# A written order for VectorE and ScalarE in the feed-forward of a two-layer encoder, and out weights split one channel tile ahead

## The chip, the cores and the metric

The kernel runs on one core of one Trainium2 chip. The metric is device time in microseconds (us) of one execution. Engines in the profile: PE is TensorE's matmul, PEld its weight load, DVE is VectorE, ACT is ScalarE, POOL is GpSimd, and SP is SyncE, which sends the DMAs. Each engine has a queue of its own, and other engines release it by semaphores.

## The reference

Two layers work on 512 frames of 1024 channels in float32. Layer 0 mixes frames with causal pooling, layer 1 with chunked attention. Each is followed by the gated feed-forward that this document is about (d_ff = 2816):

```python
def conv_ffn(h, w_gate, w_val, conv_w, conv_b, w_out):
    S = h.shape[1]
    a = h @ w_gate
    ap = jnp.pad(a, ((0, 0), (CONV_W - 1, 0), (0, 0)))
    a = ap[:, 0:S] * conv_w[0] + ap[:, 1:S + 1] * conv_w[1] + ap[:, 2:S + 2] * conv_w[2] + conv_b
    return (jax.nn.silu(a) * (h @ w_val)) @ w_out
```

## The kernel before

**Tiles.** The hidden width is cut into 22 tiles of 128 rows (`NF`). Every operand of a matmul is split into a high part (ScalarE's copy, L98) and a low part (VectorE's subtraction, L99; both are the helper `split`), and a product adds high by high, high by low and low by high. `KIND` says how a tile is made: 0 and 1 early, 2 to 4 plainly, 5 to 21 with seven half-size products of a Strassen-Winograd form in place of eight. Tile 5 (`apart`) has a form of its own, tiles 6 and 7 are narrow, and tiles 8 to 21 are "wide": a high weight part multiplies both parts of the input in one matmul of 512 columns (L603), a low part the high part in one of 256 (L605).

**A seven-product tile** (`strassen`, L579) loads its gate and value weights g and v, and VectorE makes four sums s1 to s4 of their quarters (L583 to L586). Four weight tiles are split: g1 (g itself), g2 (s2 and s3), g3 (s1 and s4) and g4 (a quarter of v). The products go in the order b11, b21, t2, t3, t1, b22, t4 and accumulate in PSUM. Between them ScalarE copies PSUM out and VectorE adds: a for the gate (L618, L624, L657, L659), val for the value (L633, L648, L649, L663), with folds (L611) of the two halves that a wide matmul leaves. At the end `hidden` runs the convolution (L417 on ScalarE, two steps L419 on VectorE), the Silu (L420), the product with val (L664) and the split of the hidden rows into one of twelve slots.

**Out-projection.** The tiles are in four groups (`OUT`: 0 to 4, 5 to 10, 11 to 16, 17 to 21). When a group's tiles are done, `output(g)` multiplies its hidden rows by the out weights for eight channel tiles d (L119 to L121) and adds to X (L678). Its matmuls are spread in threes and fours behind the products of the next group's tiles. In it, the weights of d are loaded and split just ahead of the first matmul of d; two buffers hold the parts, one the raw load of the first three groups.

**What sets the order.** PE's order is written out (`manual_schedule` with PE): the list `order` puts b22 and t4 of a tile behind b11 and b21 of the next. VectorE, ScalarE and SyncE are placed in the feed-forward by a scheduler at build time, from a model of durations and from priorities that follow the text; `high_priority` raises the copies and sums behind t1. A few other places fix VectorE and ScalarE too, and there they run in the order of the text: the stretch from `frame_rstd` to the end of `blocks` in layer 0 is one.

**Buffers that matter.** Three raw weight loads (wr), two tiles for the sums (as), three pairs of weight parts in turn (`ring`), six scratch tiles (g), four PSUM banks for the products m and t, two for b and two for the out-projection.

Of the kernel before, what the change touches and what calls it, by code (L numbers as in the profile page):

```python
# [23 lines left out]
P = 128  # L24
# [27 lines left out]

KIND = "uuppp" + "s" * 17
WIDE = range(8, NF)
OUT = ((0, 5), (5, 6), (11, 6), (17, 5))
GM = 6
WAIT, HOLD = 2, 3
# [11 lines left out]
def trunk(ctx: ExitStack, tc: tile.TileContext, xt, xT, cols, band, edge, poolw, gv, wout, wqk, wv, wo, rel, out):  # L69
# [307 lines left out]
    def ffn(l, first, pool, acc, summed=None):  # L377
# [35 lines left out]
        def hidden(f, a, finish):  # L413

            cw = [col[:, C_CW[l] + 4 * f + j:C_CW[l] + 4 * f + j + 1] for j in range(4)]
            c = g_tile(f"c{f}")
            nc.scalar.activation(c, a, AF.Identity, scale=cw[2], bias=cw[3])  # L417
            for j in range(1, 3):
                nc.vector.scalar_tensor_tensor(c[:, j:], a[:, :S - j], cw[2 - j], c[:, j:], op0=OP.mult, op1=OP.add)  # L419
            silu = nc.scalar.activation(c, c, AF.Silu)  # L420
            if l == 0 and f == NF - 1:
                with tc.issue_after(silu.ins):
                    nc.scalar.preload_act_table_set("natural_log_exp_and_others")
            finish(c)
            split(c, *slot[f])

        def early():
# [39 lines left out]
            for f in range(n):  # L467
                a = pool.tile([P, S], F32, name=f"a{f}", tag="a", bufs=2)
                with tc.issue_after(made.ins):
                    nc.vector.tensor_mul(a, o[f, 0], R)  # L470

                def finish(c):
                    nc.vector.tensor_mul(c, c, R)
                    nc.vector.tensor_mul(c, o[f, 1], c)
                hidden(f, a, finish)
            return h, seed, known, made

        B, ready = {}, {}
# [33 lines left out]
        def plain(f):  # L512

            o = []
            for i in range(2):
# [10 lines left out]
                        yield mm  # L526
                if i == 0:
                    yield mm
            hidden(f, o[0], lambda c: nc.vector.tensor_mul(c, o[1], c))
            yield mm  # L530

        def apart(f):
# [42 lines left out]
            hidden(f, a, lambda c: nc.vector.tensor_mul(c, val, c))  # L575
            yield

        def strassen(f):

            g, v = (raw_tile(f"gv{l}_{f}_{i}", gv[l, f, i]) for i in range(2))  # L580
            sa, sb = (sum_tile(f"s{x}{f}") for x in "ab")
            a11, a12, a21, a22, s2, s3, s1, s4 = (x[:, z * S:(z + 1) * S] for x in (g, v, sa, sb) for z in range(2))
            nc.vector.tensor_add(s1, a21, a22)  # L583
            nc.vector.tensor_sub(s2, s1, a11)
            nc.vector.tensor_sub(s3, a11, a21)
            nc.vector.tensor_sub(s4, a12, s2)  # L586
            wide = f in WIDE
# [4 lines left out]
            def product(o, hl, z, name, first):  # L592
# [11 lines left out]
                for i, c in enumerate(cs):  # L604
                    nc.tensor.matmul(o[:, 0], lo[:, c], B[i, name][:, 0], start=False, stop=i == 3, **how)  # L605

            def flat(o):
                return o.rearrange("p c n -> p (c n)")

            def fold(out, x):  # L610
                nc.vector.tensor_add(out, x[:, :HALF], x[:, HALF:])  # L611

            a = pool.tile([P, S], F32, name=f"a{f}", tag="a", bufs=2)
            main, side = bank("S", "m"), bank("P", "b")
            w = parts(g, 1024, f"g1_{f}")
            product(main, w, 0, "b11", True)
            if wide:
                nc.scalar.activation(a, flat(main), AF.Copy)  # L618
            else:
                nc.scalar.activation(a[:, :HALF], main[:, 0], AF.Copy)  # L620
            yield
            product(side, w, 1, "b21", True)
            if wide:
                nc.vector.tensor_add(a, a, flat(side))  # L624
                fold(a[:, :HALF], a)
            else:
                nc.vector.tensor_add(a[:, :HALF], a[:, :HALF], side[:, 0])
            yield
            val = g_tile(f"v{f}")
            w = parts(sa, 1024, f"g2_{f}")  # L630
            product(main, w, 0, "t2", False)
            if wide:
                nc.scalar.activation(val, flat(main), AF.Copy)  # L633
                fold(val[:, :HALF], val)
            else:
                nc.scalar.activation(val[:, :HALF], main[:, 0], AF.Copy)
            yield
            side = bank("S", "t")
            product(side, w, 1, "t3", True)
            yield  # L640
            w = parts(sb, 1024, f"g3_{f}")
            last = [tmp.tile([P, S], F32R, name=f"g4_{f}_{c}", tag="g", bufs=6) for c in "hl"]
            split(a22, *last)
            product(main, w, 0, "t1", False)
            with tc.high_priority():
                if wide:
                    both_ = g_tile(f"w{f}")
                    nc.scalar.activation(both_, flat(main), AF.Copy)  # L648
                    nc.vector.tensor_add(both_, both_, flat(side))  # L649
                else:  # L650
                    nc.scalar.activation(val[:, HALF:], main[:, 0], AF.Copy)
                    nc.vector.tensor_add(val[:, HALF:], val[:, HALF:], side[:, 0])
            if wide:
                fold(val[:, HALF:], both_)
            yield
            product(main, w, 1, "b22", False)
            nc.scalar.activation(a[:, HALF:], main[:, 0], AF.Copy)  # L657
# [3 lines left out]
            product(side, last, 0, "t4", False)  # L661
            for c in range(2 if wide else 1):
                nc.vector.tensor_add(val[:, :HALF], val[:, :HALF], side[:, c])  # L663
            hidden(f, a, lambda c: nc.vector.tensor_mul(c, val, c))  # L664
            yield

        def output(g):

            b, m = OUT[g]
            n = m * P  # L670
            for d in range(KD):
                w = parts(raw_tile(f"wo{l}_{g}_{d}", wout[l, d, :, b * P:(b + m) * P], n, g + 1 < len(OUT)), n, f"ow{l}_{g}_{d}", True)
                o = psum("Q", f"out{l}_{g}_{d}")
                for i in range(m):
                    s = slice(i * P, (i + 1) * P)
                    yield from mm3(o, w[0][:, s], w[1][:, s], *slot[b + i], i == 0, i == m - 1)
                for fs in (slice(0, S),) if l == 0 or g < len(OUT) - 1 or d < KD - 1 else (slice(0, HALF), slice(HALF, S)):
                    nc.vector.tensor_add(X[d][:, fs], o[:, fs], X[d][:, fs])  # L678
                    if l == 1 and g == len(OUT) - 1:
                        nc.sync.dma_start(out[d * P:(d + 1) * P, fs], X[d][:, fs])  # L680

        with tc.manual_schedule(engines={mybir.EngineType.PE}):
            h, seed, known, made = early()
            queue, left, n = [], 0, 0
            order, prev = [], None
            for f in range(NF):
                if KIND[f] == "p":
                    order += [(f, j) for j in range(8)]
                if KIND[f] == "s" and KIND[f - 1] == "p":
                    order += [(f, j) for j in range(7)]  # L690
                elif KIND[f] == "s":
                    mine = [(f, j) for j in range(5)]
                    order += [x for j in range(2) for x in (mine[j], (prev, 5 + j))] + mine[2:] if prev else mine
                    prev = f
            order += [(prev, 5), (prev, 6)]
            steps = {f: (plain if KIND[f] == "p" else strassen if KIND[f - 1] == "s" else apart)(f) for f, _ in order}
            ends = [max(x for x, (f, _) in enumerate(order) if f == b + m - 1) + 1 for b, m in OUT]
            for g, (b, m) in enumerate(OUT):
                begin = ends[g - 1] if g else 0
                points = ends[g] - begin  # L700
                hold = HOLD * 3 * OUT[g - 1][1] if g == len(OUT) - 1 else 0
                todo = left
                for at, (f, _) in enumerate(order[begin:ends[g]], 1):
                    next(steps[f])
# [4 lines left out]
                    if at > WAIT:  # L709
                        due = (todo - hold) * (at - WAIT) // (points - WAIT)  # L710
                        while todo - left < due:
                            next(queue[0])
                            left -= 1
                if g:
# [336 lines left out]
```

## Time and profile before

| | us |
|---|---|
| time, median of 3 runs | 977.11 (977.01 to 979.12) |
| the profiled execution | 977.4 |
| its span, first to last instruction | 975.6 |
| granted TensorE clock | 0.999 |

A row of the timeline gives start, duration, engine, line, operation, out<-in and, in brackets, how long the engine had been idle and what released it. A row of a group gives the count, then the union of its busy time in us and the mean duration of one in ns, then idle time before its instructions with the releasers. A row of the waits gives total us, times, and the longest. A row of a stage gives, behind the stretch, its length, then busy us and the count of each engine. Two instructions of one engine can overlap in part, so that a start-to-start distance can be below a duration.

### The profile page before, as it was taken

What the parts mean: (1) busy time and instruction counts of PE and PEld (TensorE: products, weight loads), DVE (VectorE), ACT (ScalarE), POOL (GpSimd) and SP (SyncE); (2) the same over time, 40 slices, a digit from 0 to 9 for tenths busy, and PEclk for the clock granted to TensorE, in tenths of its full rate; (3) what the DMA queues carried; (4) which work ended last, traced back from release to release, by engine and by line L of the source; (5) the groups of instructions that cost most, each with busy time, mean ns of one, the idle gap of its engine ahead of it and who ended that gap; (6) DMA issues with size and microseconds to landing.
All of it is one profiled execution on the core that took longest, in us unless ns stands there. A gap on an engine that the chain in (4) does not pass through costs nothing.

```text
span 975.6 us, 13968 instructions
## 1 busy us (share of the span) xinstructions
PE 962.5 (99%) x5038; PEld 817.7 (84%) x5038; DVE 806.1 (83%) x1452; ACT 575.5 (59%) x990; POOL 103.2 (11%) x90
## 2 busy tenths in 40 slices
PE   8999999999999999999999999999999999999998
PEld 7788988788888888888888787888998878888886
DVE  8999989999989854442777887999999999989953
ACT  7665555555555444344898988646555555565521
POOL 2300000000000013203534532000000000000000
PEclk9999999999999999999999999999999999999999
DMA  9222233232322234233343341332324323333223
GB/s 340 71 98 92 92 114 114 79 123 95 113 83 96 73 84 150 87 120 96 108 117 107 96 118 54 100 108 79 114 92 130 118 78 119 91 105 104 80 68 112
DMA packets 37429, 102.84 MB, mean 105 GB/s; under 512 B 4432, under 2 KB 7904, under 8 KB 37360
## 3 DMA queue, kind: packets, MB, share of 16 engines
q1 hardware_dynamic: 37296, 101.90, 33.0%
q8 instruction: 40, 0.66, 0.3%
q14 instruction: 29, 0.24, 0.1%
q0 software_dynamic: 32, 0.04, 0.0%
q10 hardware_dynamic: 32, 0.00, 0.0%
HBM read 95.60 MB, written 2.14 MB: 100 GB/s over the span
## 4 chain that ended last, share of the span: by engine, by line
PE 90%; DVE 7%; ACT 2%; issue 1%; DMA 1%; SPq 0%; DVEq 0%; ACTq 0%
PE st_m L603 11%; PE out L120 8%; PE out L121 8%; PE out L119 8%; PE st_m L605 5%; PE st_t L603 5%; PE gv L120 3%; PE qk L120 3%; PE qk L119 3%; PE qk L121 3%; PE gv L121 3%; PE gv L119 3%; PE st_t L605 3%; PE st_b L603 2%; PE tp L882 2%; PE oo L894 2%
## 5 line engine op out<-in xcount | busy, mean ns | idle before, releaser
L120 PE MATMUL out<-one,ow_h 128*128 128x512 f32 x224 | 88.1, 393 | 3.7 <-DVE one L99 3.7
L121 PE MATMUL out<-one,ow_l 128*128 128x512 f32 x224 | 87.8, 392 | 0.0
L119 PE MATMUL out<-one,ow_h 128*128 128x512 f32 x224 | 87.8, 392 | 0.0
L98 ACT ACTIVATE ow_h<-wo_r 128x640 fp32r<-128x640 f32 (+1 forms) x64 | 50.5, 789 | 58.6 <-PE out L120 49.3
L678 DVE TENSOR_TENSOR X<-out,X 128x512 f32<-128x512 f32 (+1 forms) x65 | 44.1, 680 | 35.7 <-PE out L121 35.7
L603 PE MATMUL st_m<-two,g_h 128*128 128x512 f32 x224 | 70.0, 394 | 0.0
L603 PE MATMUL st_m<-h,g_h 128*128 128x512 f32 x224 | 69.0, 389 | 0.0
L98 ACT ACTIVATE g_h<-gv_r 128x512 fp32r<-128x512 f32 (+1 forms) x68 | 57.3, 842 | 16.3 <-PE st_b L603 10.6
L99 DVE TENSOR_TENSOR g_l<-gv_r,g_h 128x512 fp32r<-128x512 f32 (+1 forms) x68 | 64.9, 954 | 0.0
L99 DVE TENSOR_TENSOR ow_l<-wo_r,ow_h 128x640 fp32r<-128x640 f32 (+1 forms) x64 | 56.7, 886 | 2.6 <-ACT ow_h L98 2.6
L419 DVE SCALAR_TENSOR_TENSOR c<-a,col,c 128x511 f32<-128x511 f32 (+1 forms) x76 | 56.6, 747 | 1.8 <-ACT c L417 1.8
L98 ACT ACTIVATE g_h<-sb 128x1024 fp32r<-128x1024 f32 x34 | 36.0, 1060 | 28.4 <-PE st_m L603 25.7
L121 PE MATMUL qk<-wqk_h,two 128*128 128x512 f32 x128 | 51.4, 401 | 0.0
L119 PE MATMUL qk<-wqk_h,two 128*128 128x512 f32 x128 | 50.8, 409 | 0.0
L120 PE MATMUL qk<-wqk_l,two 128*128 128x512 f32 x128 | 50.8, 397 | 0.0
L120 PEld LDWEIGHTS out<-one,ow_h 128*128 128x128 f32 x224 | 42.4, 189 | 9.8 <-DVE one L99 4.6
L99 DVE TENSOR_TENSOR g_l<-sb,g_h 128x1024 fp32r<-128x1024 f32 x34 | 41.6, 1223 | 10.4 <-ACT g_h L98 10.4
L603 PEld LDWEIGHTS st_m<-h,g_h 128*128 128x128 f32 x224 | 42.1, 188 | 9.6
L603 PEld LDWEIGHTS st_m<-two,g_h 128*128 128x128 f32 x224 | 41.6, 188 | 10.0 <-ACT w L648 0.8
L605 PEld LDWEIGHTS st_m<-two,g_l 128*128 128x128 f32 x224 | 42.0, 188 | 8.8
L121 PEld LDWEIGHTS out<-one,ow_l 128*128 128x128 f32 x224 | 42.3, 189 | 6.3
L119 PEld LDWEIGHTS out<-one,ow_h 128*128 128x128 f32 x224 | 42.3, 189 | 6.1
(370 smaller groups left out, 2921.0 us busy)
## 6 DMA issues: line engine op xcount, KB each, us to landing
gv_r<-gv SPq DMA_DIRECT2D x86, 512.0 KB, 3.5
wo_r<-wout SPq DMA_DIRECT2D x32, 384.0 KB, 3.1
wo_r<-wout SPq DMA_DIRECT2D x32, 320.0 KB, 2.9
wqk_r<-wqk SPq DMA_DIRECT2D x16, 512.0 KB, 3.4
wv_r<-wv SPq DMA_DIRECT2D x8, 512.0 KB, 3.4
wo_r<-wo SPq DMA_DIRECT2D x8, 512.0 KB, 3.4
xt<-xt SPq DMA_DIRECT2D x4, 512.0 KB, 5.8
X<-xT SPq DMA_DIRECT2D x8, 256.0 KB, 7.4
```

Source lines behind the costliest of these rows:

```text
L98: nc.scalar.activation(hi, raw, AF.Copy)
L99: return (eng or nc.vector).tensor_sub(lo, raw, hi.bitcast(F32))
L119: yield nc.tensor.matmul(o, sh, mh, start=first, stop=False, **how)
L120: yield nc.tensor.matmul(o, sh, ml, start=False, stop=False, **how)
L121: yield nc.tensor.matmul(o, sl, mh, start=False, stop=last, **how)
L419: nc.vector.scalar_tensor_tensor(c[:, j:], a[:, :S - j], cw[2 - j], c[:, j:], op0=OP.mult, op1=OP.add)
L603: nc.tensor.matmul(o, hi[:, c], B[i, name], start=first and i == 0, stop=False, **how)
L605: nc.tensor.matmul(o[:, 0], lo[:, c], B[i, name][:, 0], start=False, stop=i == 3, **how)
L678: nc.vector.tensor_add(X[d][:, fs], o[:, fs], X[d][:, fs])
L882: nc.tensor.transpose(tp[:, j * P:(j + 1) * P], s_[:, j * P:(j + 1) * P], ident)
L894: nc.tensor.matmul(oo[:, j * P:], V[j, h // 4][:, h % 4].rearrange("p a d -> p (a d)"), PT[e][c][:, 4 * j:3 * j + TT].rearrange("p t q -> ...
```

## The change

**Order.** `strassen` is cut into sixteen steps. A new generator `tour` takes steps of three tiles in turn: o is the tile before, f the tile at hand, n the next. From the first place of tile 8 to the end of tile 21 VectorE and ScalarE are under `manual_schedule` too, so that they run in the order of the text. The out-projection's instructions that are traced in this stretch fall into that order behind one of the seven places. For a wide tile it comes to this:

| place | TensorE | VectorE, in order | ScalarE, in order |
|---|---|---|---|
| 0 | b11 of f | o: w add, w fold; f: s1, s2 | o: copy w |
| 1 | b22 of o | f: s3, s4 | f: copy a, g2 high |
| 2 | b21 of f | o: add second half of a; f: g2 low | o: copy second half of a, convolution start |
| 3 | t4 of o | f: a add, a fold; o: two convolution steps | f: g3 high; o: Silu |
| 4 | t2 of f | o: two val adds; f: g3 low | |
| 5 | t3 of f | f: val fold; o: product with val, hidden low | f: copy val; o: hidden high; n: g1 high |
| 6 | t1 of f | n: g1 low; f: g4 low | f: g4 high |

The loads of g and v of the next tile are traced at place 3. Tiles 6 and 7 take their steps in the same order, but the scheduler places them. `high_priority` is gone.

**Out weights.** `output` loads and splits the weights of channel tile d + 1 ahead of the matmuls of d, and those of its first channel tile as soon as its group is at hand.

```diff
+ORDERED = 8
...
             nc.scalar.activation(c, a, AF.Identity, scale=cw[2], bias=cw[3])
+            yield
             for j in range(1, 3):
                 nc.vector.scalar_tensor_tensor(c[:, j:], a[:, :S - j], cw[2 - j], c[:, j:], op0=OP.mult, op1=OP.add)
             silu = nc.scalar.activation(c, c, AF.Silu)
...
+            yield
             finish(c)
             split(c, *slot[f])
...
+            *w1, lo = parts(g, 1024, f"g1_{f}", later=True)
+            yield
+            lo()
+            yield
+            sa, sb = (sum_tile(f"s{x}{f}") for x in "ab")
+            a11, a12, a21, a22, s2, s3, s1, s4 = (x[:, z * S:(z + 1) * S] for x in (g, v, sa, sb) for z in range(2))
+            nc.vector.tensor_add(s1, a21, a22)
+            nc.vector.tensor_sub(s2, s1, a11)
+            main, side = bank("S", "m"), bank("P", "b")
+            product(main, w1, 0, "b11", True)
+            yield
             a = pool.tile([P, S], F32, name=f"a{f}", tag="a", bufs=2)
+            copy(a, main)
+            nc.vector.tensor_sub(s3, a11, a21)
+            nc.vector.tensor_sub(s4, a12, s2)
+            *w2, lo = parts(sa, 1024, f"g2_{f}", later=True)
+            yield
+            lo()
+            product(side, w1, 1, "b21", True)
+            yield
+            add(a, side)
+            fold(a[:, :HALF], a)
+            *w3, lo = parts(sb, 1024, f"g3_{f}", later=True)
+            yield
+            lo()
+            product(main, w2, 0, "t2", False)
             yield
             val = g_tile(f"v{f}")
+            copy(val, main)
+            fold(val[:, :HALF], val)
             side = bank("S", "t")
+            product(side, w2, 1, "t3", True)
+            yield
+            w4 = [tmp.tile([P, S], F32R, name=f"g4_{f}_{c}", tag="g", bufs=6) for c in "hl"]
+            split(a22, *w4)
+            product(main, w3, 0, "t1", False)
+            yield
+            x = g_tile(f"w{f}") if wide else val[:, HALF:]
+            copy(x, main)
+            add(x, side)
+            fold(val[:, HALF:], x)
+            yield
+            product(main, w3, 1, "b22", False)
+            yield
             nc.scalar.activation(a[:, HALF:], main[:, 0], AF.Copy)
             if wide:
                 nc.vector.tensor_add(a[:, HALF:], a[:, HALF:], main[:, 1])
+            gate = hidden(f, a, lambda c: nc.vector.tensor_mul(c, val, c))
+            next(gate)
+            yield
+            next(gate)
+            product(side, w4, 0, "t4", False)
+            yield
             for c in range(2 if wide else 1):
                 nc.vector.tensor_add(val[:, :HALF], val[:, :HALF], side[:, c])
+            yield
+            run(gate)
             yield
...
+            load(0)
+            yield
             for d in range(KD):
+                if d + 1 < KD:
+                    load(d + 1)
...
+                    now, new = new, strassen(f + 1) if f + 1 < NF else None
+                    for k, who in enumerate(("of", "fo", "of", "fon", "of", "fon", "nf")):
+                        if f == ORDERED and k == 0:
+                            order.enter_context(tc.manual_schedule(engines={ET.DVE, ET.Activation}))
+                        for x in who:
+                            if step := {"o": old, "f": now, "n": new}[x]:
+                                next(step)
+                        if old or k not in (1, 3):
+                            yield
+                    old = now
+            for k in range(6):
+                next(old)
+                if k in (1, 3):
+                    yield
+            order.close()
...
                 queue.append(output(g))
+                next(queue[0])
```

`parts(..., later=True)` gives the high part's copy at once and the low part's subtraction as a function to call later.

More of the change, by code (lines that the diff above doesn't have):

```diff
@@ L474, in finish @@
                     nc.vector.tensor_mul(c, o[f, 1], c)
-                hidden(f, a, finish)
+                run(hidden(f, a, finish))
             return h, seed, known, made
@@ L528, in plain @@
                     yield mm
-            hidden(f, o[0], lambda c: nc.vector.tensor_mul(c, o[1], c))
+            run(hidden(f, o[0], lambda c: nc.vector.tensor_mul(c, o[1], c)))
             yield mm
@@ L574, in apart @@
             nc.vector.tensor_add(val[:, :HALF], val[:, :HALF], product(w, 0, "t4"))
-            hidden(f, a, lambda c: nc.vector.tensor_mul(c, val, c))
+            run(hidden(f, a, lambda c: nc.vector.tensor_mul(c, val, c)))
             yield
         def strassen(f):
+            wide = f in WIDE
             g, v = (raw_tile(f"gv{l}_{f}_{i}", gv[l, f, i]) for i in range(2))
[L581 to L587, printed above, removed]
+            yield
             def bank(tag, name):
@@ L607, in flat, with fold @@
+            def fold(out, x):
+                if wide:
+                    nc.vector.tensor_add(out, x[:, :HALF], x[:, HALF:])
             def flat(o):
                 return o.rearrange("p c n -> p (c n)")
-            def fold(out, x):
-                nc.vector.tensor_add(out, x[:, :HALF], x[:, HALF:])
-            a = pool.tile([P, S], F32, name=f"a{f}", tag="a", bufs=2)
-            main, side = bank("S", "m"), bank("P", "b")
-            w = parts(g, 1024, f"g1_{f}")
-            product(main, w, 0, "b11", True)
@@ L629, in strassen @@
             val = g_tile(f"v{f}")
[L630 to L636, printed above, removed]
+            copy(val, main)
+            fold(val[:, :HALF], val)
+            side = bank("S", "t")
+            product(side, w2, 1, "t3", True)
             yield
-            side = bank("S", "t")
@@ L680, in output, with tour @@
                         nc.sync.dma_start(out[d * P:(d + 1) * P, fs], X[d][:, fs])
+        def tour():
+            for f in range(NF):
+                if KIND[f] == "p":
+                    yield from plain(f)
+                elif KIND[f] == "s" and KIND[f - 1] == "p":
+                    old, new = None, strassen(f + 1)
+                    for j, _ in enumerate(apart(f)):
+                        if j in (3, 5, 6):
+                            next(new)
+                        yield
+                elif KIND[f] == "s":
+                    now, new = new, strassen(f + 1) if f + 1 < NF else None
[13 more added lines that the diff above has]
+            order.close()
         with tc.manual_schedule(engines={mybir.EngineType.PE}):
@@ L684, in ffn @@
             queue, left, n = [], 0, 0
-            order, prev = [], None
+            order = ExitStack()
+            seq = []
             for f in range(NF):
[L687 to L697, printed above, removed]
+                if KIND[f] == "s" and KIND[f - 1] == "s":
+                    old = [[(f - 1, z)] if KIND[f - 2] == "s" else [] for z in (False, True)]
+                    seq += [(f, False), *old[0], (f, False), *old[1], *[(f, False)] * 3]
+                elif KIND[f] != "u":
+                    seq += [(f, z == 1) for z in range({"p": 8, "s": 7}[KIND[f]], 0, -1)]
+            seq += [(NF - 1, False), (NF - 1, True)]
+            ends = [seq.index((b + m - 1, True)) + 1 for b, m in OUT]
+            steps = tour()
             for g, (b, m) in enumerate(OUT):
-                begin = ends[g - 1] if g else 0
-                points = ends[g] - begin
+                points = ends[g] - (ends[g - 1] if g else 0)
                 hold = HOLD * 3 * OUT[g - 1][1] if g == len(OUT) - 1 else 0
                 todo = left
-                for at, (f, _) in enumerate(order[begin:ends[g]], 1):
-                    next(steps[f])
+                for at in range(1, points + 1):
+                    next(steps)
                     if n in range(3, 20, 5):
@@ L713, in ffn @@
                             left -= 1
+                if g == len(OUT) - 1:
+                    run(steps)
                 if g:
```

44 lines of the change are left out of this document (14 added, 30 removed).

## The prediction

> **What bounds the kernel now.** I began with the busy times and slices of the page.
>
> ```profile
> span 975.6 us, 13968 instructions
> ...
> PE 962.5 (99%) x5038; PEld 817.7 (84%) x5038; DVE 806.1 (83%) x1452; ACT 575.5 (59%) x990; POOL 103.2 (11%) x90
> ...
> PE   8999999999999999999999999999999999999998
> ...
> DVE  8999989999989854442777887999999999989953
> ```
>
> TensorE (PE) is busy 962.5 of 975.6 us and sets the time. VectorE (DVE) averages 83%, but the slices show that this mixes two things: 9 in both feed-forwards, 4 to 8 in the attention between them. So I asked for the stage that the change orders. In layer 0 it runs from the first matmul of tile 8 to the last of t1 of tile 21:
>
> ```profile
> 125.56 0.63 PE L603 MATMUL st_m<-two,g_h 128*128 128x512 f32 x2
> ...
> 332.72 0.40 PE L605 MATMUL st_m<-h,g_l 128*128 128x256 f32 x2
> ```
>
> Layer 1 has the same stretch 594 us later. Both as stages; columns: length, then busy time of PE, its weight load, DVE, ACT and POOL.
>
> ```profile
> 125.50:333.00 207.50, 205.65 (x1091) 176.36 (x1091) 191.89 (x308) 116.18 (x169) 0.00 (x0) 1.00 0.32 101
> 719.50:927.00 207.50, 205.65 (x1092) 176.34 (x1091) 192.03 (x308) 116.44 (x169) 0.00 (x0) 1.00 0.32 101
> ```
>
> PE idles 1.85 us here. VectorE has 191.9 us of work in 207.5 us, so its room is 15.6 us, some 7.5%. That is the number to keep in mind: an order that makes VectorE stand idle for longer than its room turns it into the bound. Next, what PE waits for, from the view of waits, and the place in the timeline:
>
> ```profile
> PE out L120 <- DVE one L99: 3.7, 2, 1.9
> ```
>
> ```profile
> 190.12 0.40 PE L121 MATMUL out<-one,ow_l 128*128 128x512 f32 x1
> ...
> 190.36 0.40 PE L119 MATMUL out<-one,ow_h 128*128 128x512 f32 x1
> 191.87 0.69 DVE L99 TENSOR_TENSOR one<-c,one 128x512 fp32r<-128x512 f32 x1
> 192.61 0.50 PE L120 MATMUL out<-one,ow_h 128*128 128x512 f32 x1 [1.85 <-DVE one L99]
> ```
>
> This is all that PE loses in the two stretches but for hundredths: once a layer the out-projection of tile 10 wants the low part of tile 10's hidden rows, and VectorE makes it at 191.87. Two such matmuls start 0.24 us apart (190.12 and 190.36), the stalled one 2.25 us behind, so the loss is 2.02 us a layer. **The most that the change can gain is therefore 4.0 us.**
>
> **What goes.** In the new order the low part of tile 10 stands at place 5 of tile 11 (table in the section on the change); the matmul that wants it comes at place 3 of tile 12. The 2.02 us go in both layers; nothing is late behind them, since the next matmul of the projection starts at once today. The instructions themselves stay: the same products, copies, adds and splits, and the same loads. PE's own order doesn't change either: both texts give b11, b22 of the tile before, b21, t4 of the tile before, t2, t3, t1.
>
> **What the fixed order costs VectorE.** That such a stretch is run as written shows where the kernel has one now:
>
> ```profile
> 44.91 0.16 DVE L152 TENSOR_SCALAR f_a<-f_st 128x4 f32<-128x4 f32 x1
> 44.99 1.23 DVE L406 TENSOR_TENSOR gv_l<-gv_r,gv_h 128x1024 fp32r<-128x1024 f32 x1
> 46.14 0.16 DVE L133 SCALAR_TENSOR_TENSOR f_t<-f_y 128x4 f32<-128x4 f32 x1
> ```
>
> L152, the handed-in subtraction L406, then L133 of the next helper: the order of the text. So I walk the table for one steady tile, with VectorE behind (that it gets behind is the result of the sum). Two things cost it time: neighbours that depend on one another, and trips to ScalarE with nothing between. The prices:
>
> ```profile
> 189.53 0.69 DVE L583 TENSOR_TENSOR sb<-gv_r 128x512 f32<-128x512 f32 x1
> 190.13 0.69 DVE L585 TENSOR_TENSOR sa<-gv_r,gv_r 128x512 f32<-128x512 f32 x1
> ...
> 331.46 0.69 DVE L664 TENSOR_TENSOR c<-v,c 128x512 f32<-128x512 f32 x1 [0.16 <-ACT c L420]
> 332.85 0.69 DVE L99 TENSOR_TENSOR one<-c,one 128x512 fp32r<-128x512 f32 x1 [0.70 <-ACT one L98]
> 333.79 0.69 DVE L649 TENSOR_TENSOR w<-w,st_t 128x512 f32<-128x512 f32 x1 [0.24 <-ACT w L648]
> 334.51 0.42 DVE L611 TENSOR_TENSOR v<-w 128x256 f32<-128x256 f32 x1
> ```
>
> Two independent adds start 0.60 us apart, though each takes 0.69: they overlap. The fold L611 reads what L649 wrote and starts 0.72 behind it. **A dependent neighbour costs 0.12.** The new order has five such pairs a tile: w add and its fold, s1 and s2, a add and its fold, the two convolution steps, the two val adds: 0.60 us a tile.
>
> The Trainium skill ("VectorE: DVE Perf Modes", The DRAIN you can't avoid) says that the next VectorE operation waits until the pipe is empty anyway and that a semaphore between two adds nothing. These rows disagree, 0.60 against 0.72. By that rule dependent and independent pairs cost the same, the 0.60 us a tile fall away, and the sum is the one of the second rival below.
>
> The second pair of rows is a round trip: the gate's product, ScalarE's copy, the low part. It starts 1.39 us behind the product where a neighbour would start 0.60 behind, so it costs 0.79 (B). At place 5 the text has exactly this, with nothing between. The other two trips need ScalarE's durations and the distance of two of its starts:
>
> ```profile
> L98 ACT ACTIVATE g_h<-gv_r 128x1024 fp32r<-128x1024 f32 x13 | 13.8, 1059 | 5.6 <-PE st_b L603 5.2 <-ACT ow_h L98 0.5
> L98 ACT ACTIVATE ow_h<-wo_r 128x768 fp32r<-128x768 f32 x14 | 11.8, 840 | 7.6 <-PE out L120 7.4
> L420 ACT ACTIVATE c<-c 128x512 f32<-128x512 f32 x14 | 8.8, 626 | 5.3 <-DVE c L419 5.3
> L98 ACT ACTIVATE one<-c 128x512 fp32r<-128x512 f32 x11 | 6.9, 625 | 1.6 <-DVE c L664 1.6
> L657 ACT ACTIVATE a<-st_m 128x256 f32<-128x256 f32 x14 | 5.1, 366 | 0.0
> ```
>
> ```profile
> 227.61 1.06 ACT L98 ACTIVATE g_h<-sa 128x1024 fp32r<-128x1024 f32 x1
> 228.58 0.62 ACT L420 ACTIVATE c<-c 128x512 f32<-128x512 f32 x1
> ```
>
> ScalarE starts 0.97 us behind the start of a 1.06 us copy, so 0.1 ahead of its end. B's idle 0.70 is the 0.63 us copy and 0.07 for the two handovers, 0.04 and 0.03.
>
> - A, places 1 and 2: the high part of g2 can't start before s3 ends, and the copy of a's second half stands behind it on ScalarE, and VectorE's add of that half behind that. From the start of s3: 0.69 + 0.04 + 0.97 + 0.37 + 0.03 = 2.10 us. VectorE has only s3 and s4 to do, 1.20. A costs 0.90.
> - C, places 5 and 6: g1's high part for the next tile stands behind the hidden rows' copy. From the gate's product: 0.69 + 0.04 + 0.53 + 1.06 + 0.03 = 2.35, where VectorE is ready at 1.39 + 0.60 = 1.99. C costs 0.36.
>
> Together 0.60 + 0.79 + 0.90 + 0.36 = 2.65 us a tile, 37.1 for 14 tiles. All three trips begin and end on VectorE, so that it is late doesn't hide them.
>
> The out weights' part and the addition to X now stand at fixed points too, after any of the seven places. X's addition (0.60 from start to start) hides most of ScalarE's 0.84 us. After place 3 ScalarE has the Silu first, and VectorE waits 0.08 + 0.04 + 0.53 + 0.84 + 0.03 - 0.60 = 0.92 (0.08 being the overlap that the conv step's end still has to run); after place 5 it costs 0.14 and after place 1 it fills 0.12 of A; elsewhere nothing. Mean 0.13, and this row counts 17 of them:
>
> ```profile
> L678 DVE TENSOR_TENSOR X<-out,X 128x512 f32<-128x512 f32 x17 | 11.7, 685 | 0.0
> ```
>
> That is 2.3 us, with 0 and 17 x 0.92 = 15.6 as its ends.
>
> **The sum for a layer.** 191.9 (busy) + 37.1 + 2.3 = 231.3 us. Tile 7, narrow, finishes in tile 8's places without folds and without the second half's add: 0.7 less. t1 of tile 21 needs only g3's low part of place 4; behind that VectorE has 0.34 + 0.60 + 0.79 + 0.60 + 0.60 = 2.9 us left, and PE needs 0.6 to end the product: 2.3 less. So 228.3 us in place of 207.5, while PE's own need is 207.5 - 2.0 = 205.5: **VectorE becomes the bound**, and the stretch grows by 20.8 us, the 2.0 gained already in it. Two layers: 41.6. The profiled execution took 977.4 us, its span and 1.8 around it; the median of the runs shown is 977.1, 0.3 below. 977.4 + 41.6 = **1019.0 us**.
>
> **What I cost at nothing.** Loads: each tile's two are traced at place 3, two places of some 2 us ahead of their first reader, and land in 3.5 us by this row:
>
> ```profile
> gv_r<-gv SPq DMA_DIRECT2D x86, 512.0 KB, 3.5
> ```
>
> If SyncE sends them no earlier, the reader on ScalarE, g1's high part, waits at most a few tenths, and the wait falls beside VectorE's lag. An out load is traced one channel tile, some 10 us, ahead of its use on PE. Tiles 6 and 7 stay with the scheduler but are traced differently:
>
> ```profile
> 90.00:125.50 35.50, 35.42 (x251) 33.11 (x250) 34.83 (x54) 20.57 (x32) 0.00 (x0) 1.00 0.36 116
> ```
>
> PE can win 0.1 us there; VectorE's idle is 0.7, so another order may cost something. I take 0, with the largest wait seen, 1.9 a layer, as the other end. The last out group is scheduled as before and PE's matmuls follow each other there; 0.
>
> **Rivals.**
> - *The order fits* (12%). PE stays the bound if the added idle time stays under 205.5 - 191.9 = 13.6 us a layer, 0.97 a tile. Only the stall goes: 977.4 - 4.0 = 973.4. For it: VectorE idles 15.6 us today without harm, and a fixed order need add no waits where PE paces. Against it: A and B alone are 1.69 a tile, and B is measured.
> - *Dependent neighbours cost nothing* (9%): they would overlap like the others, 0.60 x 14 = 8.4 less a layer, 1019.0 - 16.8 = 1002.2. Against it: 0.72 beside 0.60 above. (The rule of the Trainium skill, "VectorE: DVE Perf Modes", The DRAIN you can't avoid, comes to this price.)
> - *Only A and B are real* (8%): C and the out waits are covered as well; 5.0 + 2.3 less a layer on top: 1002.2 - 14.6 = 987.6.
> - *The out parts wait everywhere* (6%): 13.3 more a layer, 1045.6. VectorE meets the place 3 case one time in seven, which speaks against it.
> - *Nothing changes* (4%): the given order comes out as good or bad as the scheduler's; 977.
>
> **How the numbers follow.** The forecast has 61%, with 1000 to 1038 for the unknown ends. Slower by over 0.2% (2 us, about what a measurement of this kernel can tell from no change) is the forecast and three rivals: 84%; within it 4%; faster 12%. A range from 985 to 1040 leaves out the faster case, the unchanged one and most of the dearest: about 2 in 10.
>
> **What would show it.** In PE's waits: the products' matmuls with low weight parts (g_l) held by VectorE's splits, some 1 to 2 us a tile, and the row with `one` gone. VectorE's waits: on ScalarE's copy of a's half 0.8 to 0.9 us, on the hidden rows' copy 0.7, on g1's high part 0.3, fourteen times a layer each. VectorE's span from tile 8 to 21 near 228 us with 192 us busy. I'm wrong if PE's stretch stays within 2 us of 205, or if those three waits are missing while VectorE still works to the end.

## The result, and the profile after

The changed kernel takes 1030.12 us (median of 4 runs, 1029.36 to 1030.67) where the kernel before, run beside it, takes 977.40 (977.01 to 979.12): 1.0535 times as long, 95% interval 1.0517 to 1.0554. The forecast was 1019.0 with a range of 985 to 1040. The profiled execution took 1029.4 us, 52.0 more than that of before, and its span grew by the same 52.0. Lines that had moved by one or a few are easy to match: `split` is now L99 and L100, the products' high and low weight parts are L601 and L603, the split through `parts` is L406 and L407.

The page of the changed kernel, its busy times, two rows of slices and the shares of the chain that ended last:

```profile
span 1027.6 us, 13793 instructions
...
PE 983.9 (96%) x5038; PEld 818.3 (80%) x5038; DVE 823.2 (80%) x1452; ACT 570.7 (56%) x990; POOL 103.2 (10%) x90
...
PE   9999999899999899999999999999999899988998
...
DVE  8999888888888855452677888999888888888853
...
PE 49%; DVE 37%; ACT 10%; issue 3%; DMA 0%; DVEq 0%; ACTq 0%
```

The shares of the chain in the kernel before:

```profile
PE 90%; DVE 7%; ACT 2%; issue 1%; DMA 1%; SPq 0%; DVEq 0%; ACTq 0%
```

In both feed-forwards PE now has eights among its nines, and VectorE eights where it had nines. VectorE's share went down, from 83 to 80%, while it became the bound. That is the trap in a share: VectorE has the same 1452 instructions, but it stands idle for others in a longer span. What shows the change of bound is the chain, where VectorE and ScalarE together hold 47% of the span in place of 9%.

The stretch from tile 8 to t1 of tile 21 in both layers, as stages (length, then busy PE, weight load, VectorE, ScalarE, POOL, the granted clock, the DMA share and GB/s):

```profile
125.00:358.00 233.00, 218.57 (x1093) 178.69 (x1092) 201.40 (x309) 113.53 (x168) 0.00 (x0) 0.97 0.29 89
745.40:978.10 232.70, 214.25 (x1093) 174.38 (x1092) 201.33 (x309) 113.37 (x168) 0.00 (x0) 1.00 0.29 90
```

The stretch was 207.5 us in both layers and is 233.0 and 232.7, so 50.7 of the 52.0 us are here. VectorE's busy time is 201.4 against 191.9 for the same work, and the other 31.6 us of the 233.0 it stands still. PE's busy time went up by 13 us in layer 0 and by 9 in layer 1 with the same matmuls; their ends are modelled, and in layer 0 some ran at a lower clock (last section), so that busy is no measure of its work here.

PE's longest waits in the changed kernel:

```profile
PE st_m L601 <- ACT g_h L406: 14.9, 16, 1.3
PE st_m L603 <- DVE g_l L407: 13.7, 12, 1.7
...
PE st_m L601 <- ACT w L607: 2.3, 2, 1.2
```

The row with `one`, 3.7 us for tile 10's hidden rows, is gone. In its place PE waits 28.6 us for the high and low weight parts of the next product, 28 times, up to 1.7 us each, and a few more for ScalarE's copies of v and w. Who made those parts late stands in VectorE's waits, whole span. These are the lines that belong to the stretch; two waits in each of the first three lie outside of it:

```profile
DVE a L671 <- ACT a L669: 20.7, 26, 0.8
...
DVE one L100 <- ACT one L99: 14.0, 20, 0.7
DVE ow_l L100 <- ACT ow_h L99: 14.0, 18, 1.1
...
DVE g_l L407 <- ACT g_h L406: 6.7, 24, 0.5
```

All four are waits for a copy on ScalarE, an engine that is busy for 113.5 of 233.0 us. The hidden rows have four other names besides `one` (u0l to u3l) with 1.4 us each, so their row is 19.6 us in 28 waits. How one tile looks on VectorE, from the timeline:

```profile
236.19 0.69 DVE L672 TENSOR_TENSOR c<-v,c 128x512 f32<-128x512 f32 x1
237.57 0.69 DVE L100 TENSOR_TENSOR u2l<-c,u2h 128x512 fp32r<-128x512 f32 x1 [0.70 <-ACT u2h L99]
...
239.25 0.96 DVE L100 TENSOR_TENSOR ow_l<-wo_r,ow_h 128x768 fp32r<-128x768 f32 x1 [0.39 <-ACT ow_h L99]
...
241.86 0.68 DVE L613 TENSOR_TENSOR w<-w,st_t 128x512 f32<-128x512 f32 x1
242.58 0.42 DVE L619 TENSOR_TENSOR v<-w 128x256 f32<-128x256 f32 x1
242.92 0.69 DVE L631 TENSOR_TENSOR sb<-gv_r 128x512 f32<-128x512 f32 x1
243.64 0.69 DVE L632 TENSOR_TENSOR sa<-sb,gv_r 128x512 f32<-128x512 f32 x1
244.25 0.68 DVE L638 TENSOR_TENSOR sa<-gv_r,gv_r 128x512 f32<-128x512 f32 x1
244.86 0.68 DVE L639 TENSOR_TENSOR sb<-gv_r,sa 128x512 f32<-128x512 f32 x1
246.34 0.42 DVE L671 TENSOR_TENSOR a<-a,st_m 128x256 f32<-128x256 f32 x1 [0.80 <-ACT a L669]
```

Here stand the prediction's trips B (0.70 idle ahead of the low part of the hidden rows), an out weights' part (0.39) and A (0.80 ahead of the add of a's second half), and two of the dependent pairs: the fold starts 0.72 behind the add, s2 0.72 behind s1, where s3 and s4 start 0.61 behind what stands ahead of them.

### The profile page after: what moved, and what is told of

Same layout as the page of the kernel before. It is cut to its first block, busy times and chain, and to the rows that moved or that the text cites. A ratio compares the mean times of both kernels' runs of the same rounds, so it can differ in the third digit from the quotient of the medians.

```text
span 1027.6 us, 13793 instructions
## 1 busy us (share of the span) xinstructions
PE 983.9 (96%) x5038; PEld 818.3 (80%) x5038; DVE 823.2 (80%) x1452; ACT 570.7 (56%) x990; POOL 103.2 (10%) x90
## 4 chain that ended last, share of the span: by engine, by line
PE 49%; DVE 37%; ACT 10%; issue 3%; DMA 0%; DVEq 0%; ACTq 0%
DVE g_l L407 8%; ACT g_h L406 5%; DVE c L421 4%; PE out L121 4%; PE out L122 4%; PE out L120 4%; DVE ow_l L100 3%; PE gv L121 3%; PE qk L121 3%; PE qk L120 3%; PE qk L122 3%; PE gv L122 3%; PE gv L120 3%; DVE v L679 2%; DVE v L619 2%
## 5 line engine op out<-in xcount | busy, mean ns | idle before, releaser
L601 PE MATMUL st_m<-two,g_h 128*128 128x512 f32 x224 | 74.7, 415 | 20.5 <-ACT g_h L406 14.9
L99 ACT ACTIVATE ow_h<-wo_r 128x640 fp32r<-128x640 f32 (+1 forms) x64 | 50.2, 784 | 43.8 <-PE out L121 35.7
L406 ACT ACTIVATE g_h<-sa 128x1024 fp32r<-128x1024 f32 x32 | 34.0, 1061 | 72.1 <-DVE sa L638 65.2
L601 PEld LDWEIGHTS st_m<-two,g_h 128*128 128x128 f32 x224 | 40.4, 192 | 40.4 <-ACT g_h L406 25.3
L601 PE MATMUL st_m<-h,g_h 128*128 128x512 f32 x224 | 70.3, 395 | 0.0
L603 PEld LDWEIGHTS st_m<-two,g_l 128*128 128x128 f32 x224 | 40.1, 190 | 34.8 <-DVE g_l L407 28.2
L100 DVE TENSOR_TENSOR ow_l<-wo_r,ow_h 128x640 fp32r<-128x640 f32 (+1 forms) x64 | 56.7, 885 | 14.0 <-ACT ow_h L99 14.0
L603 PE MATMUL st_m<-two,g_l 128*128 128x256 f32 x224 | 48.2, 298 | 14.8 <-DVE g_l L407 13.7
L422 ACT ACTIVATE c<-c 128x512 f32<-128x512 f32 x44 | 27.6, 630 | 58.8 <-DVE c L421 58.7
L601 PEld LDWEIGHTS st_m<-h,g_h 128*128 128x128 f32 x224 | 42.9, 192 | 9.9
L99 ACT ACTIVATE one<-c 128x512 fp32r<-128x512 f32 x28 | 17.6, 629 | 53.0 <-DVE c L672 51.8
```

The lines of the kernel that those rows point to most:

```text
L99: nc.scalar.activation(hi, raw, AF.Copy)
L100: return (eng or nc.vector).tensor_sub(lo, raw, hi.bitcast(F32))
L406: nc.scalar.activation(hi[:, :n], raw[:, :n], AF.Copy)
L601: nc.tensor.matmul(o, hi[:, c], B[i, name], start=first and i == 0, stop=False, **how)
```

## The experiments

The theory: each tile's fixed order contains trips from VectorE to ScalarE and back with too little VectorE work inside (A, B, C and the out weights), and neighbours that depend on one another. In one queue nothing else can fill these holes, so VectorE becomes the bound. The rivals: it is not the order but what else came with the new text (the loads and splits of the out weights one channel tile ahead, `high_priority` gone); or dependent neighbours are free and the trips are all of it. Times are medians; ratios stand against the kernel before on the same chip (977.51 us for the first four, 978.33 for the others). What a run brings back is counted from the changed kernel's 1030.1 us, measured beside another set of runs; counted by the ratios it comes out within 0.4 us of the same. No run puts VectorE alone or ScalarE alone under the fixed order, so which of the two engines' orders does how much of it stays open.

**1. The new text, all of it under the scheduler**

```diff
-ORDERED = 8
+ORDERED = NF
```

> The changed kernel without the written order: VectorE and ScalarE go back to the scheduler in all tiles; the new cut into steps, the earlier traced loads, the missing high_priority and the out weights one channel tile ahead stay. Theory (the idle time that the written order gives VectorE is the whole loss): 971 to 980 us, within 0.5% of before, VectorE idle some 15 us in the 207 us from tile 8 to t1 of tile 21. Rival (the text's new order, the missing priority or the earlier out parts cost the time): 1000 us or more.

978.17 us, ratio 1.0001 [0.9993, 1.0010]. Without the given order of VectorE and ScalarE the loss is gone; the sixteen steps, the missing priority and the earlier out weights together change nothing beyond 1 us. PE's first wait in this run is the old one:

```profile
PE out L121 <- DVE one L100: 3.7, 2, 1.9
```

So the out weights' lookahead did not take that stall away either; the order did.

**2. The fixed order, with the out weights split just ahead of their matmuls, as before**

```diff
-            load(0)
-            yield
             for d in range(KD):
-                if d + 1 < KD:
-                    load(d + 1)
+                load(d)
...
                 queue.append(output(g))
-                next(queue[0])
```

> The changed kernel with the out weights of channel tile d loaded and split just ahead of the matmuls of d, as before; the written order stays. Theory (written order): no gain, 1025 us or more, and rather worse, 1030 to 1060, since PE's next matmul then needs a split that stands at the end of VectorE's lag. Rival (the out parts one channel tile ahead are the cost): back to 977 to 985 us.

1066.27 us, ratio 1.0904 [1.0889, 1.0919]: 36 us slower still, and more than I expected. PE's first two waits:

```profile
PE out L120 <- ACT ow_h L99: 40.8, 22, 3.0
PE out L122 <- DVE ow_l L100: 17.1, 22, 1.9
```

PE's waits for the products' parts have given way to waits for the out weights' parts, 44 times. The two halves of the change belong together: the lookahead is worth nothing under the scheduler (run 1), which finds room for those splits by itself, and 36 us under a fixed order, which puts them where the text has them.

**3. The fixed order from tile 15 on**

```diff
-ORDERED = 8
+ORDERED = 15
```

> The written order from tile 15 on in place of tile 8, so on 7 tiles of a layer in place of 14; nothing else changes. Theory (each ordered tile costs VectorE the same idle time, and PE's pace is passed from the first on): about half the loss, 1000 to 1008 us. Rival (a cost of the switch from scheduler to written order, paid once a layer): 1025 to 1030 us. Rival (the loss sits in tiles 8 to 14, with five-row and six-row out groups): under 990 us.

1009.63 us, ratio 1.0323 [1.0307, 1.0339], 1.6 us above what I expected, and far from what both rivals asked for (1025 to 1030 us, under 990). The half without the order is as before but for a slower clock, the half with it carries the loss; the same run's stages:

```profile
125.00:230.00 105.00, 103.15 (x543) 88.34 (x542) 95.29 (x152) 57.98 (x85) 0.00 (x0) 0.98 0.30 99
230.00:345.00 115.00, 107.39 (x542) 88.24 (x541) 97.90 (x151) 55.78 (x82) 0.00 (x0) 0.99 0.28 89
```

In the first PE idles 1.85 us, which is tile 10's stall; t1 of tile 21 ends behind the second, at 347.6 us. The loss grows with the tiles under the order: 32.1 us for seven tiles a layer, 52.7 for fourteen. That half of them have 61% of it is the miss. A part of it is the stall: this run keeps it and the full change wins it back, 2.0 us a layer, so that the order itself costs 52.7 + 4.0 = 56.7 us there and 32.1 here, 57%. Layer 0's timelines have most of the rest: from t1 of tile 14 to t1 of tile 21 this run takes 117.55 us where the kernel before takes 104.13, 13.4 us for seven tiles, and the full change, counted in the same way, takes 25.2 us and the 2.0 of the stall for fourteen, so that the tiles alone come to 49%. On top of them stand costs that don't go by tiles: PE's wait for w behind tile 21 (2.3 us in this run as in the full change), and 1.6 us that the half without the order lost here at a lower clock behind tile 10's stall (granted 0.53 from 193.0 to 196.5 us; last section).

**4. Trip A alone: more work between g2's high part and the add that it holds up**

```diff
             nc.vector.tensor_add(s1, a21, a22)
+            nc.vector.tensor_sub(s3, a11, a21)
             nc.vector.tensor_sub(s2, s1, a11)
...
             copy(a, main)
-            nc.vector.tensor_sub(s3, a11, a21)
...
-for k, who in enumerate(("of", "fo", "of", "fon", "of", "fon", "nf")):
+for k, who in enumerate(("fo", "fo", "of", "fon", "of", "fon", "nf")):
```

Place 0 becomes s1, s3, s2, then the tile before's w add and fold. VectorE does w's add, its fold and s4 while ScalarE copies.

> At place 0 the sums s1, s3, s2 stand ahead of w add and fold, s4 stays at place 1: the high part of g2 then starts 1.1 us earlier against VectorE, so VectorE has w add, fold and s4 to do while ScalarE copies. Theory (three round trips and five dependent pairs add up on VectorE): the 0.8 us wait for the copy of a's second half goes in nearly all tiles, with the pair s1, s2: 12 x 0.88 + 14 x 0.12 = 12 us a layer, 24 in all, 1004 to 1010 us. Rival (PE's clock or PE's own waits set the pace, VectorE's waits are cover): 1025 us or more.

1003.22 us, ratio 1.0260 [1.0246, 1.0274]: 26.9 us back by moving one subtraction and one step, 0.8 us better than expected. VectorE's wait for a's half in this run:

```profile
DVE a L671 <- ACT a L669: 1.6, 2, 0.8
```

19.1 us less idle in 24 waits; each wait also cost the 0.09 us by which two operations overlap when they are not held (2.2), and s1 and s2 are no longer neighbours (28 times 0.12, 3.4). That makes 24.7 of the 26.9. Of the other waits the out weights' shrank (14.0 to 12.2) and g1's grew as much (6.7 to 8.7), so that some 2 us of the gain stay without an account.

**5. Trips B and C alone: the split of the hidden rows cut in two, g1's high part ahead of it**

```diff
-            split(c, *slot[f])
+            hi, lo = slot[f]
+            nc.scalar.activation(hi, c, AF.Copy)
+            yield
+            nc.vector.tensor_sub(lo, c, hi.bitcast(F32))
...
-for k, who in enumerate(("of", "fo", "of", "fon", "of", "fon", "nf")):
+for k, who in enumerate(("of", "fo", "of", "fon", "of", "fno", "nof")):
```

> At places 5 and 6 g1's high part for the next tile stands ahead of the hidden rows' high part on ScalarE, and g1's low part between the gate's product and the hidden rows' low part on VectorE. Theory (the idle times on VectorE add up): the waits of 0.70 (13 a layer) and 0.28 (12 a layer) go, with their overlaps 13 x 0.78 + 12 x 0.36 = 14.5 us a layer, 29 in all: 999 to 1006 us. Rival (VectorE's waits are cover for PE's own): 1025 us or more.

1004.75 us, ratio 1.0272 [1.0258, 1.0286], 25.4 us back. Its waits on VectorE for the trips:

```profile
DVE a L674 <- ACT a L672: 22.0, 26, 2.1
...
DVE ow_l L100 <- ACT ow_h L99: 16.3, 18, 1.4
...
DVE one L431 <- ACT one L429: 2.8, 4, 0.7
...
DVE g_l L407 <- ACT g_h L406: 1.1, 2, 0.5
```

B falls from 28 waits to 4 and C from 24 to 2, the others stay and grow a little (by 1.3 and 2.3): the trips don't hide in one another.

**6. The dependent pairs alone: another tile's operation between each two**

The pairs w add and fold, s1 and s2, a add and fold, the two convolution steps and the two val adds are cut by a `yield`, and the tour goes to the other tile between:

```diff
-for k, who in enumerate(("of", "fo", "of", "fon", "of", "fon", "nf")):
+for k, who in enumerate(("ofof", "fo", "of", "fofon", "ofo", "fon", "nf")):
```

> The five dependent pairs of a tile are put apart by one independent VectorE instruction each (w add, s1, fold, s2; a add, first convolution step, fold, second step; val add, g3's low part, val add); the round trips to ScalarE stay. Theory (a dependent neighbour costs 0.12 us): some 65 pairs a layer, 7.7 us, 15 in all: 1013 to 1018 us. Rival (VectorE drains after every instruction anyway, so that pairs cost nothing): 1028 to 1032 us.

1012.97 us, ratio 1.0359 [1.0345, 1.0373], 17.2 us back, while the four waits on ScalarE stay as they were, as these rows of its waits show:

```profile
DVE a L674 <- ACT a L672: 20.7, 26, 0.8
...
DVE ow_l L100 <- ACT ow_h L99: 14.3, 18, 1.3
DVE one L100 <- ACT one L99: 14.0, 20, 0.7
DVE g_l L407 <- ACT g_h L406: 6.6, 24, 0.5
```

In its timeline the same four instructions as above now start every 0.60 us:

```profile
238.38 0.68 DVE L613 TENSOR_TENSOR w<-w,st_t 128x512 f32<-128x512 f32 x1
238.98 0.68 DVE L631 TENSOR_TENSOR sb<-gv_r 128x512 f32<-128x512 f32 x1
239.58 0.42 DVE L619 TENSOR_TENSOR v<-w 128x256 f32<-128x256 f32 x1
239.91 0.68 DVE L633 TENSOR_TENSOR sa<-sb,gv_r 128x512 f32<-128x512 f32 x1
```

The rival by which dependent neighbours are free falls: 28 tiles times 0.60 us is 16.8, and 17.2 came back. The rule of the Trainium skill ("VectorE: DVE Perf Modes", The DRAIN you can't avoid), that the next operation has to wait for the pipe anyway and a semaphore costs nothing extra, does not hold for these float32 operations of 256 to 512 columns. The section adds that an operation which is not held starts earlier; here it is the dependence on the neighbour that decides, 0.60 us from start to start without it and 0.72 with it.

**7. The out weights' low part three matmuls behind their high part**

`load` splits into the high copy at once and a function for the low part:

```diff
-                if d + 1 < KD:
-                    load(d + 1)
+                late = load(d + 1) if d + 1 < KD else None
...
+                    if i == 1 and late:
+                        late()
```

> The low part of the out weights stands three matmuls behind its high part, so that it falls to the next place of the order and VectorE doesn't wait there for ScalarE. Theory: the 18 waits of 0.78 us (14 us in the two layers) go, 1014 to 1019 us. Rival (that wait is cover for a later one): 1026 us or more.

1017.78 us, ratio 1.0407 [1.0393, 1.0421], 12.3 us back. The wait of the out weights in this run:

```profile
DVE ow_l L407 <- ACT ow_h L406: 6.1, 6, 1.3
```

7.9 us less idle and 12 overlaps of 0.09 are 9.0. The rest is in waits that shrank with it: the add that waits for b21 (2.4 to 0.9 us), g1's high part (6.7 to 5.1) and a's half (20.7 to 19.4), less 0.7 for the hidden rows, where it grew.

**8. All four of them: 4 to 7 in one kernel**

```diff
-for k, who in enumerate(("of", "fo", "of", "fon", "of", "fon", "nf")):
+for k, who in enumerate(("fofo", "fo", "of", "fofon", "ofo", "fno", "nof")):
```

with the edits of 4 to 7 in the steps themselves.

> The edits of the four runs before it together (sums first, hidden rows apart, pairs apart, out low part later), with the written order from tile 8 on. Theory (a written order costs only by its idle times): VectorE needs 191 to 194 us of the stretch again, PE's 205.5 us set the pace, the stall at tile 10 stays away: 972 to 975 us, faster than before by 0.2 to 0.5%. Rival (a fixed order is slower by itself, whatever stands next to what): 985 us or more.

974.66 us (974.57 to 975.16, 6 runs), ratio 0.9965 [0.9953, 0.9977]: faster than the changed kernel by 55.5 us and, by the ratio, than the kernel before by 3.4 (2.3 to 4.6). Layer 0's stretch in this run:

```profile
125.80:332.00 206.20, 206.15 (x1091) 176.18 (x1091) 193.76 (x309) 117.62 (x170) 0.00 (x0) 1.00 0.32 101
```

PE works for 206.15 of 206.20 us: it is the bound again, with neither tile 10's stall nor a wait for a weight part. The four savings alone sum to 26.9 + 25.4 + 17.2 + 12.3 = 81.8 us, and together they give 55.5. This is the floor that PE sets: below its own need there is nothing to win, however much more room VectorE has. The prediction had named 4.0 us as the most that the change can gain. From the first matmul of tile 8 to the last of t1 of tile 21, start to start, this profile has 205.8 us in layer 0 where the kernel before has 207.2, so 1.4 of the 2.0 us a layer came and the rest was not traced. The last section has a likely reason why the ratio shows more than twice 1.4.

## Why the prediction was right, and where it was short

**Right: the mechanism.** A fixed order turns VectorE into the bound of this stretch; run 1 shows that the loss goes with the order, runs 4 to 7 that it is the holes which the prediction lists, and run 8 that nothing else of weight is left. Its signs came as named: the row with `one` gone, PE held by the splits up to 1.7 us, the three waits of VectorE with 0.80, 0.70 and 0.3 us. One came otherwise: VectorE is busy for 201.4 us and not 192, since what two operations no longer overlap counts as busy.

**Short: 11 us, by the size of one term and two small ones that it lacked.** The terms for one layer, measured in layer 0's stretch with VectorE's waits of that stretch alone:

```profile
DVE a L671 <- ACT a L669: 9.5, 12, 0.8
DVE one L100 <- ACT one L99: 6.3, 9, 0.7
DVE ow_l L100 <- ACT ow_h L99: 5.9, 8, 0.9
DVE g_l L407 <- ACT g_h L406: 3.3, 12, 0.5
DVE a L613 <- PE st_b L603: 1.4, 2, 1.1
...
DVE u3l L100 <- ACT u3h L99: 0.7, 1, 0.7
```

With each wait goes the lost overlap of 0.09 us, so 12 waits of trip A cost 9.5 + 1.1. For B, the rows of `one` and of u0l to u3l are 9.1 us in 13 waits.

| term, us a layer | forecast | measured |
|---|---|---|
| dependent pairs | 14 x 0.60 = 8.4 | 68 starts x 0.12 = 8.2 |
| trip A | 14 x 0.90 = 12.6 | 12 waits, 10.6 |
| trip B | 14 x 0.79 = 11.1 | 13 waits, 10.3 |
| trip C | 14 x 0.36 = 5.0 | 12 waits, 4.4 |
| out weights' parts | 17 x 0.13 = 2.3 | 8 waits, 6.6 |
| wait for PE's b21 | 0 | 2 waits, 1.6 |
| tile 7 and behind t1 of tile 21 | -3.0 | in the counts above |
| sum | 36.4 | 41.7 |

Measured, the stretch is 233.0 - 191.9 = 41.1 us longer than VectorE's work, so the list is complete to 0.6.

- *The prices were right.* A, B and C cost 0.89, 0.79 and 0.36 apiece, as worked out from the rows of before. Only the counts are a little lower.
- *The step that failed is the out weights' term, "VectorE meets the place 3 case one time in seven".* Of the 17 parts in the stretch 5 fall behind the convolution steps of place 3 and wait 0.89 each, 2 behind place 5 (0.39) and 1 behind s4 (0.66). One such case of place 3:

```profile
354.14 0.96 DVE L100 TENSOR_TENSOR ow_l<-wo_r,ow_h 128x768 fp32r<-128x768 f32 x1 [0.90 <-ACT ow_h L99]
```

  I had taken an even spread over seven places. The text doesn't spread them evenly: the parts follow the steps of the tour, and where they fall can be counted in it. That was 4.3 us a layer, 8.6 of the 11. The price of that case, 0.92 with the overlap in it, was 0.98.
- *Waits for PE and ScalarE were left out.* VectorE waits twice for PE's b21 in this stretch:

```profile
130.88 0.69 DVE L613 TENSOR_TENSOR a<-a,st_b 128x512 f32<-128x512 f32 x1 [1.09 <-PE st_b L603]
...
248.15 0.69 DVE L613 TENSOR_TENSOR a<-a,st_b 128x512 f32<-128x512 f32 x1 [0.26 <-PE st_b L603]
```

  The first is in tile 8, where VectorE isn't behind yet; the sum had it behind from the first place on. And b22 of tile 21 waits for the copy of w behind the stretch (2.3 us in 2 waits), a hand-over to the rest that the prediction had at nothing.
- *A detail of the sign was too narrow.* The prediction had PE wait for low parts, VectorE's splits. Half of its wait is for a high part on ScalarE (14.9 us in 16 waits), whose copy stands behind VectorE's work too (ScalarE waits 65.2 us, 28 times, for s3 ahead of such copies). It is the same lag, seen on another engine.
- *Costs at nothing that were nothing.* Run 1 bears out tiles 6 and 7 and the earlier out loads; no wait for a DMA of g and v is in the stretch's list of VectorE's waits.

**The rivals.** That the order fits, and that nothing changes, fell in the result, but run 8 shows how near the first was: with the same queues, the same instructions and another interleaving it does fit, and the time is 974.7 where that rival said 973.4. Free neighbours fell in run 6, "only A and B" by trip C's 12 waits a layer and run 7. The dearest, out parts waiting everywhere, was too dear: 8 of 17 waited.

## What to carry to other kernels

When an in-order engine sends work to another engine and reads the answer, count the independent work that stands between the two in its own queue: each trip costs the other engine's time less that work, here in 12 or 13 of 14 tiles, as soon as the engine's room is used up. A fixed order wants the trip's two ends cut into steps of their own and other tiles' operations put between, dependent neighbours too; here four moves of that kind turned 53 us of loss into 3 of gain without one instruction less. What is traced into such an order from elsewhere, like the out weights here, must be counted place by place, since an average over places hides the one that waits.

## What the runs showed of the hardware that I had not expected

Behind some stalls, and not behind others, TensorE runs at about half its speed for 3 to 7 us. From the changed kernel's timeline of PE:

```profile
241.40 0.69 PE L603 MATMUL st_m<-two,g_l 128*128 128x256 f32 x2 [1.67 <-DVE g_l L407]
...
242.32 0.63 PE L121 MATMUL out<-one,ow_h 128*128 128x512 f32 x1
242.75 0.63 PE L122 MATMUL out<-one,ow_l 128*128 128x512 f32 x1
...
245.64 0.40 PE L121 MATMUL out<-one,ow_h 128*128 128x512 f32 x1
245.87 0.40 PE L122 MATMUL out<-one,ow_l 128*128 128x512 f32 x1
```

The same matmuls of 512 columns start 0.43 us apart and then, from about 245 us on, 0.23. The granted clock says the same: it is 0.97 for layer 0's stretch, which has three such pieces, from 187, 241 and 289 us on. Yet it cost next to nothing here: layer 1's stretch shows 1.00 and is 232.7 us long where layer 0's is 233.0. VectorE was the bound in both, and PE, when slow, only waited less; the one place where VectorE felt it is probably the 0.26 us at 248.15 above, soon behind the slow matmuls.

Where PE is the bound it costs time, and tile 10's stall shows both outcomes. The kernel before had a gap of 1.85 us at 190.76, and the matmuls behind it, from 192.94 on, started 0.24 us apart. Run 1 has the same gap in the same place, and this is the stage behind it:

```profile
193.00:196.50 3.50, 3.50 (x12) 2.94 (x11) 3.50 (x7) 1.88 (x4) 0.00 (x0) 0.53 0.00 0
```

The granted clock is 0.53 where the kernel before has 1.00 in the same 3.5 us. The same matmuls, from the held one to the first of the next t1, take 6.54 us in run 1 and 4.97 in the kernel before, so that the stall cost 1.6 us more than the 2.0 that the prediction gave it. That is probably what sets the runs of one kernel apart: of the ten runs of the kernel before that run 8 is compared with, the four with a granted clock of 0.997 or 0.998 took 979.0 to 979.3 us and the six with 1.000 took 977.2 to 978.4, while run 8, without the stall, took 974.6 to 975.2 in all six.

So the length of the last gap doesn't settle it. The Trainium skill ("TensorE: Matmul & The Clock Gate", Part 1: The HAM clock gate) says that the array falls to half its clock after an idle window of some 3.4 us and that the windows run freely. The half speed agrees, 0.43 against 0.23; but the gap in run 1 is 1.85 us and no single gap of the changed kernel's stretch is longer than 1.7, so here it took less than a whole window of idle time. Which stalls bring it stays open.
